# Two-layer pooling and attention backbone: the first gate's conditioning as four 1 MB pieces between the mixer's groups, and the first MLP weights cast in two halves

## The chip, the core and the metric

The kernel runs on one core of one Trainium2 chip. The metric is the device time of one execution in microseconds (us); the median of three runs before the change is 1172.9 us (1172.45 to 1174.26).

Five engines work side by side, each in the order of its own instruction list: PE (matmul), PEld (the weight loads of PE), DVE (vector), ACT (scalar), POOL, and SP, which here only issues transfers. They wait for each other by semaphores.

## The reference, cut to what matters

Two layers over 512 latent and 256 context rows of width 1024. Every sub-layer is modulated by shift, scale and gate vectors that a linear map makes out of a conditioning vector. Layer 0 mixes tokens by centred means, layer 1 by attention; each is followed by a squared-ReLU MLP.

```python
def ada_mods(cond, w, b):
    m = (jax.nn.silu(cond) @ w + b)[..., None, :]
    return jnp.split(m, N_MOD, axis=-1)          # sh1, sc1, gt1, sh2, sc2, gt2
...
        h_lat = modulate(rms_norm(x, g_mix_pre[i]), sh1, sc1)
...
            y_lat = pool_mixer(h_lat, w_pool[j], pool_scale[j])
...
        x = x + gt1 * rms_norm(y_lat, g_mix_post[i])
        m_lat = sq_relu_mlp(modulate(rms_norm(x, g_mlp_pre[i]), sh2, sc2), w_mlp_in[i], w_mlp_out[i])
```

## The kernel before, in words

Rows are kept in six tiles of 128 (tiles 0 to 3 latent, 4 and 5 context). Every large product is made of three fp32r matmuls (high by high, high by low, low by high), so each operand is split: ACT casts it to fp32r (the high part) and DVE subtracts that from the original (the low part). The helper `split` does this.

The first 100 us are the first stage: layer 0's norm, conditioning, pooling mixer, gate and residual, and the first part of the MLP. It is a list of steps with times written out by hand (class `Steps`, `st.at(time, function, ...)`); the list is sorted by time and the functions called in that order. The times are only an order: up to 48 (PE) and 47.3 (DVE, ACT) the engines keep exactly the order of the list (line 65 in the profile); behind that a scheduler may reorder, by its own estimate of durations.

The conditioning of layer 0 is read from HBM in 1 MB blocks (`raw_load`, line 123, issued by SP in list order) into four buffers. For each piece three steps follow:

- `ada_mm` (line 219) multiplies the blocks with the conditioning vector, into one PSUM bank `psada`. A piece of width 4 has two blocks, each with four matmuls of 128 x 512 that fill the four 32-row quarters of the bank (in the trace each such fp32 matmul is two records); width 2 has one block with eight matmuls of 128 x 256.
- `ada_rows` transposes the bank on DVE into `work` or `rows`.
- `ada_sel` sums and turns it by four small matmuls (`work,sel` or `rows,sel`) into the same bank, and `ada_out` adds the bias on DVE into `mods`. Only then is the bank free.

The bank comes from the pool `psB` of four banks, which the context part of the centred means (`psc`), the context mixer's results (`pspool`, tile 4), the gate rows (`psg`) and transposes (`psx`) share. A buffer of a 1 MB block is free again when its last matmul has read it.

The mixer: `centred` makes the operands `ra` (ACT high, DVE low) for eight column blocks k, `pool_a(t, (g,))` does the six 128 x 256 matmuls of tile t and group g (k = 2g, 2g+1) into `pspool`. The gate GT1 then goes through `gate_rows`: DVE multiplies `mods` by a gain into `gc`, four matmuls spread it over the rows (`psg`), ACT copies that to `gate`. DVE multiplies it into the mixer's result (line 326) and adds to the residual stream `xr` (line 329).

After that, per tile pair: `turn0` transposes on PE (`psx`, line 379), `mod0` applies shift and scale on ACT (line 389) and DVE (line 391) and splits (ACT line 395, DVE line 396), and `parts0` does the first MLP product (`psin`, line 567). The first MLP weights arrive in one 1 MB block; before, one `split` makes `rb` of all 2048 columns (ACT line 142, DVE line 145). From about 125 us on the MLP runs in groups on PE (lines 817 and 691).

What the change touches: the body of `ada_mm`, the loop over `CONDITIONING` that puts these steps in the list, one time of the second piece of SC2/SH2 (`landing`), and the step of `split(*raws[0])`.

Of the kernel before, what the change touches and what calls it, by code (L numbers as in the profile page):

```python
# [9 lines left out]
F32 = mybir.dt.float32  # L10
# [7 lines left out]
P = 128  # L18
D = 1024
KT = D // P  # L20
# [14 lines left out]
SH1, SC1, GT1, SH2, SC2, GT2 = range(6)  # L35
# [33 lines left out]
def backbone(ctx: ExitStack, tc, x, ctx_in, w_ada, w_pool, pool_scale, w_qkv, g_q, g_k, w_o, w_mlp_in,  # L69
# [21 lines left out]
    psB = ctx.enter_context(tc.tile_pool(name="psB", bufs=4, space=PSUM))  # L91
# [29 lines left out]
    def raw_load(src, pool=None):  # L121
        t = (pool or pools[0]).tile([P, 2048], F32, tag="raw", name="raw")
        d = sy.dma_start(t, src)
        if pinned[0]:
            tc.keep_in_program_order(d)
        return t
# [12 lines left out]
    def split(raw, hi, lo, pin=False, q=None):  # L139
        if q is not None:  # L140
            raw, hi, lo = (z[:, 512 * q:512 * q + 512] for z in (raw, hi, lo))
        a = sc.copy(hi, raw)  # L142
        if pin:
            tc.keep_in_program_order(a)
        b = ve.tensor_tensor(out=lo, in0=raw, in1=hi, op=ALU.subtract)  # L145
        if pin:
            tc.keep_in_program_order(b)
# [68 lines left out]

    rowsd, parts, seeded, stale = {}, {}, {}, [0]

    def ada_mm(i, m, j, w=2):
        ps = psB.tile([P, 512], F32, tag="b", name="psada")  # L220
        kn = 2048 // (w * P)
        for z in range(KT // kn):
            raw = raw_load(w_ada[i, m, j + z]).rearrange("p (k n) -> p k n", n=w * P)
            for k in range(kn):
                at = kn * z + k
                q = 32 * (at % 4)
                te.matmul(ps[q:q + 32, 0:w * P], cond[:, at, :], raw[:, k, :], start=(at < 4), stop=(at >= 4))  # L227
        rowsd[i, m, j] = ps, w

    def ada_rows(i, m, j):  # L230
        ps, w = rowsd[i, m, j]
# [489 lines left out]
    def w_in(i, g, rg, pin=False, wait=None):  # L721
        return rg.load(w_mlp_in[i, g], 256, pin, wait)
# [4 lines left out]
    st = Steps()  # L727
    for t in range(NT):
        st.at(4.6 + 1.3 * t, rows_a, t)
    landing = ((19.3, 21.4, 22.4), (23.8, 25.9, 27), (27.1, 28.15, 28.7), (28.9, 30.0, 30.5), (31.4, 32.4, 33.4),  # L730
               (33.7, 34.8, 35.2), (40.6, 42.65, 43.9), (44.2, 46.25, 47.2),
               (47.75, 48.5, 49.5), (52.8, 53.2, 54.7), (60.5, 61.5, 62), (62.9, 63.9, 64.4), (65.2, 66.2, 66.7), (67.7, 68.7, 69.2))
    for zs, (m, j, w) in zip(landing, CONDITIONING):
        for z, fn, also in zip(zs, (ada_mm, ada_rows, ada_sel), ((w,), (), ())):
            st.at(z, fn, 0, m, j, *also)
    st.at(0, ordered.__setitem__, 0, True)
    st.at(0, mixed.__setitem__, 0, True)
    st.at(47.3, mixed.__setitem__, 0, False)
# [25 lines left out]
        st.at((23.4, 24.4)[h], pool_split, h, False)  # L764
    raws = []
    st.at(62.95, lambda: first.append(Inner(0, w_in(0, 0, ring, False, raws), hH, hL, hids0[0], chunks0, TOK)))
    st.at(63.2, lambda: split(*raws[0]))
    for h in range(2):
        for ci in range(2):
            st.at(((47.65, 46.2), (47.7, 47.6))[h][ci], gate_rows, 0, GT1, ci, (h,))  # L770
# [4 lines left out]
    for n, t in enumerate(order):  # L775
        b = 50.5 + 2.9 * n
# [685 lines left out]
```

## Time and profile before

| what | value |
|---|---|
| median of three runs | 1172.9 us |
| the profiled execution's own time / its span | 1173.48 / 1171.7 us |
| PE busy in the span | 1143.0 us (98%) |
| DVE, ACT, POOL busy | 938.4, 636.7, 67.0 us |
| mean granted PE clock | 0.996 of full |
| PE busy, 30 to 40 / 40 to 50 / 50 to 60 us | 7.48 / 9.30 / 9.42 of 10 us |
| PE clock in the same stretches | 0.97 / 0.69 / 1.00 |

A row of the timeline gives the start in us, the time until the last of the merged instructions ended, engine, line, operation, output and inputs, shapes, how many records, and in brackets the idle time before it with what ended it. Records of matmuls overlap, so the time a group takes on PE is read from its start to the start of the next group. Line 65 stands for every step whose order is pinned.

### The profile page before, as it was taken

To read this page: it belongs to the slowest core of one execution; us is meant where nothing else is said; L and a number is where in the kernel's file an instruction comes from. 1 tells how busy PE (TensorE), PEld (TensorE's weight loads), DVE (VectorE), ACT (ScalarE), POOL (GpSimd) and SP (SyncE) were. 2 spreads that over 40 slices of the span, in tenths; PEclk is the share of its full clock that TensorE was granted. 3 is DMA by queue.
4 is the path that set the end of the run, shared out by engine and by line. 5 is a ranking of instruction groups with operands and counts; after the bars stand their busy time and mean duration, and the time that the engine had idled before them with its cause. 6 is when DMAs were issued, how large, how long until landed. Compare 5 with 4: busy or idle time off the path is not lost.

```text
span 1171.7 us, 15966 instructions
## 1 busy us (share of the span) xinstructions
PE 1143.0 (98%) x6172; PEld 989.2 (84%) x6172; DVE 938.4 (80%) x1538; ACT 636.7 (54%) x1082; POOL 67.0 (6%) x120
## 2 busy tenths in 40 slices
PE   7899999999999999999999999999899999999997
PEld 5579899889899988998887889988888888888886
DVE  4688687989988997996778599877787779778876
ACT  4577655555454534555675388852776436535522
POOL 2030000000000000000241200001100000000001
PEclk9899999999999999999999999999999999999999
DMA  9884213343334334343423101115234124314312
GB/s 375 354 318 154 72 45 135 133 159 109 144 144 144 144 137 147 112 144 108 180 73 107 37 1 37 37 73 197 91 138 150 61 84 144 108 36 144 108 37 107
DMA packets 25516, 147.32 MB, mean 126 GB/s; under 512 B 2785, under 2 KB 5217, under 8 KB 9698
## 3 DMA queue, kind: packets, MB, share of 16 engines
q1 hardware_dynamic: 25442, 146.32, 34.2%
q8 instruction: 48, 0.79, 0.3%
q14 instruction: 26, 0.21, 0.1%
HBM read 138.96 MB, written 7.34 MB: 125 GB/s over the span
## 4 chain that ended last, share of the span: by engine, by line
PE 49%; issue 42%; POOL 3%; DVE 2%; ACT 2%; DMA 1%; SPq 0%; POOLq 0%; DVEq 0%; ACTq 0%
PE pso L817 22%; PE psin L691 18%; PE psin L567 3%; PE psq L1064 2%; PE pspool L65 1%; POOL rs L185 1%; PE psada L65 1%; PE pspool L490 1%; POOL rs L1073 1%; DMA raw<-in_w_ada 1%; DMA xr<-in_x 1%; PE psada L227 1%; POOL ms L183 1%; DVE ra L65 0%; ACT junk L170 0%
## 5 line engine op out<-in xcount | busy, mean ns | idle before, releaser
L817 PE MATMUL pso<-units,rb 128*128 128x512 f32 x1152 | 278.2, 392 | 0.0
L817 PEld LDWEIGHTS pso<-units,rb 128*128 128x128 f32 x1152 | 214.8, 188 | 41.2
L273 DVE SCALAR_TENSOR_TENSOR rows<-raw,cond,rows 128x256 f32<-128x256 f32 x280 | 126.5, 475 | 2.0
L829 DVE TENSOR_TENSOR acc<-acc,pso 128x512 f32<-128x512 f32 x129 | 85.1, 674 | 41.4 <-PE pso L817 41.2
L567 PE MATMUL psin<-ra,rb 128*128 128x512 f32 (+1 forms) x432 | 103.3, 340 | 1.8 <-ACT ra L364 1.6
L921 PE MATMUL pso<-units,pairs 128*128 128x512 f32 x336 | 82.3, 389 | 0.0
L567 PE MATMUL psin<-ra 128*128 128x512 f32 x256 | 80.5, 390 | 0.0
L567 PEld LDWEIGHTS psin<-ra,rb 128*128 128x128 f32 x432 | 69.9, 189 | 11.3 <-ACT ra L364 1.9
L921 PEld LDWEIGHTS pso<-units,pairs 128*128 128x128 f32 x336 | 63.1, 188 | 13.1
L925 DVE TENSOR_TENSOR acc<-acc,pso 128x512 f32<-128x512 f32 x72 | 48.7, 681 | 28.8 <-PE pso L921 28.8
L183 POOL TENSOR_SCALAR ms<-ss 128x1 f32<-128x1 f32 x20 | 11.4, 572 | 998.3 <-ACT junk L170 946.1
L691 PE MATMUL psin<-ra,units 128*128 128x384 f32 x336 | 65.5, 337 | 0.4 <-ACT psin L703 0.4
L691 PE MATMUL psin<-sums,units 128*128 128x384 f32 x336 | 63.9, 337 | 0.0
L691 PEld LDWEIGHTS psin<-ra,units 128*128 128x128 f32 x336 | 59.7, 188 | 3.9 <-ACT psin L703 0.9
L691 PEld LDWEIGHTS psin<-sums,units 128*128 128x128 f32 x336 | 58.9, 188 | 1.7
L145 DVE TENSOR_TENSOR units<-raw,units 128x1024 fp32r<-128x1024 f32 (+2 forms) x49 | 55.1, 1148 | 4.5 <-ACT units L142 4.4
L567 PEld LDWEIGHTS psin<-ra 128*128 128x128 f32 x256 | 48.0, 188 | 10.0
L142 ACT CAST units<-raw 128x1024 fp32r<-128x1024 f32 (+2 forms) x49 | 46.8, 994 | 14.0 <-PE pso L817 10.2
L827 ACT COPY acc<-pso 128x512 f32<-128x512 f32 x48 | 27.2, 588 | 48.9 <-PE pso L817 48.6
L567 PE MATMUL psin<-rb 128*128 128x512 f32 (+1 forms) x144 | 52.6, 367 | 0.2 <-DVE rb L365 0.2
L1064 PE MATMUL psq<-units,ra 128*128 128x512 f32 x216 | 51.7, 392 | 0.0
L567 PE MATMUL psin<-rb,ra 128*128 128x512 f32 x128 | 49.8, 389 | 0.0
(279 smaller groups left out, 2346.7 us busy)
## 6 DMA issues: line engine op xcount, KB each, us to landing
raw<-in_w_ada SPq DMA_DIRECT2D x48, 1024.0 KB, 4.9
raw<-in_w_mlp_in SPq DMA_DIRECT2D x32, 1024.0 KB, 4.9
raw<-in_w_mlp_out SPq DMA_DIRECT2D x32, 1024.0 KB, 5.3
raw<-in_w_qkv SPq DMA_DIRECT2D x6, 1024.0 KB, 4.8
spill<-xr SPq DMA_DIRECT2D x10, 512.0 KB, 4.2
xr<-spill SPq DMA_DIRECT2D x10, 512.0 KB, 6.8
raw<-in_w_o SPq DMA_DIRECT2D x4, 1024.0 KB, 4.8
xr<-in_x SPq DMA_DIRECT2D x4, 512.0 KB, 5.2
```

The lines of the kernel that those rows point to most:

```text
L65: return lambda *args, **kw: self.tc.keep_in_program_order(f(*args, **kw))
L142: a = sc.copy(hi, raw)
L145: b = ve.tensor_tensor(out=lo, in0=raw, in1=hi, op=ALU.subtract)
L273: ve.scalar_tensor_tensor(out=r, in0=raw[:, k, :], scalar=cond[:, k, c:c + 1], in1=r, op0=ALU.mult, op1=ALU.add)
L567: te.matmul(ps[:, bank, o:o + ln], w[:, k, fs], rhs, start=start, stop=(k == KT - 1 and n == 2), skip_group_check=len(ks) < KT)
L691: te.matmul(bank, w[k], a[k], start=start and k == 0 and m == 0, stop=stop and k == 3 and m == 2, skip_group_check=True)
L817: te.matmul(pss[h][:, 0:cols[h][1]], a[:, f, ts_], w[:, f, cols[h][0]:sum(cols[h])], start=(n == 0 and not seeded[t]), stop=(n == len(seq) ...
L827: sc.copy(d, ps)
L829: ve.tensor_tensor(out=d, in0=d, in1=ps[:, 0:w], op=ALU.add)
L921: te.matmul(ps, a, w, start=(m == 0), stop=(m == len(seq) - 1))
L925: ve.tensor_tensor(out=M[n][:, t], in0=M[n][:, t], in1=ps, op=ALU.add)
L1064: te.matmul(ps, a[:, k, sl], w[:, k % 4, :], start=(k == 0 and n == 0), stop=(k == KT - 1 and n == 2))
```

## The change

For the gate GT1 (two pieces of width 4, so four blocks) `ada_mm` is no longer called once per piece with both blocks, but once per block. The first piece's blocks stand at 35.3 and 36.25 in the list, the second's at 40.6 and 42.61; before, the two whole pieces stood at 40.6 and 44.2. `ada_rows` and `ada_sel` stay where they were (42.65 and 43.9; 46.25 and 47.2). The whole piece SH2 of columns 0 to 511 moves from 52.8 to 52.5 in the list. The split of the first MLP weights becomes two steps of 1024 columns. Bytes, matmuls and their operands stay the same; ACT and DVE have one instruction more each.

```diff
-    def ada_mm(i, m, j, w=2):
-        ps = psB.tile([P, 512], F32, tag="b", name="psada")
-        kn = 2048 // (w * P)
-        for z in range(KT // kn):
+    def ada_mm(i, m, j, w=2, zs=None):
+        if (i, m, j) not in rowsd:
+            rowsd[i, m, j] = psB.tile([P, 512], F32, tag="b", name="psada"), w
+        ps, kn = rowsd[i, m, j][0], 2048 // (w * P)
+        for z in range(KT // kn) if zs is None else zs:
             raw = raw_load(w_ada[i, m, j + z]).rearrange("p (k n) -> p k n", n=w * P)
...
-        rowsd[i, m, j] = ps, w
...
-               (47.75, 48.5, 49.5), (52.8, 53.2, 54.7), (60.5, 61.5, 62), (62.9, 63.9, 64.4), (65.2, 66.2, 66.7), (67.7, 68.7, 69.2))
+               (47.75, 48.5, 49.5), (52.5, 53.2, 54.7), (60.5, 61.5, 62), (62.9, 63.9, 64.4), (65.2, 66.2, 66.7), (67.7, 68.7, 69.2))
     for zs, (m, j, w) in zip(landing, CONDITIONING):
         for z, fn, also in zip(zs, (ada_mm, ada_rows, ada_sel), ((w,), (), ())):
-            st.at(z, fn, 0, m, j, *also)
+            if m != GT1 or fn != ada_mm:
+                st.at(z, fn, 0, m, j, *also)
+        if m == GT1:
+            for z in range(2):
+                st.at(((35.3, 36.25), (40.6, 42.61))[j // 2][z], ada_mm, 0, m, j, w, (z,))
...
-    st.at(63.2, lambda: split(*raws[0]))
+    for h in range(2):
+        st.at((63.2, 63.55)[h], lambda h: split(*(z[:, 1024 * h:1024 * h + 1024] for z in raws[0])), h)
```

On PE, in the pinned part, the mixer's groups and the gate stood like this before (`pspool` the mixer, `psada<-raw` the blocks of GT1, `psada<-work,sel` their turning, `psg` the gate rows):

```order
L65 MATMUL pspool<-rb,ra 128x256 x24
L65 MATMUL psada<-raw,cond 32x512 x8
L65 MATMUL pspool<-rb,ra 128x256 x12
L65 MATMUL psada<-work,sel 32x2x4 x4
L65 MATMUL psada<-raw,cond 32x512 x8
L65 MATMUL psg<-ident,gc 128x128 x4
L65 MATMUL psada<-work,sel 32x2x4 x4
L65 MATMUL psg<-ident,gc 128x128 x12
```

The same place on PE with the change:

```order
L65 MATMUL psada<-raw,cond 32x512 x4
L65 MATMUL pspool<-rb,ra 128x256 x12
L65 MATMUL psada<-raw,cond 32x512 x4
L65 MATMUL pspool<-rb,ra 128x256 x12
L65 MATMUL psada<-raw,cond 32x512 x4
L65 MATMUL pspool<-rb,ra 128x256 x6
L65 MATMUL psada<-raw,cond 32x512 x4
L65 MATMUL pspool<-rb,ra 128x256 x6
L65 MATMUL psada<-work,sel 32x2x4 x4
L65 MATMUL psg<-ident,gc 128x128 x4
L65 MATMUL psada<-work,sel 32x2x4 x4
L65 MATMUL psg<-ident,gc 128x128 x12
```

All four blocks now stand ahead of the last mixer group, and between the first turning and the first `psg` nothing is left; before, eight block matmuls stood there. The first block takes the bank that `psc` of k = 4, 5 leaves, the mixer's second bank that of the last SH1 piece; before, the mixer had the former and GT1 the latter.

Some 10 us later on PE, where the order is the scheduler's, the piece SH2 (line 227) before stood whole behind tile 1's mixer (line 490):

```order
L490 MATMUL pspool<-rb,ra 128x256 x8
L238 MATMUL psada<-work,sel 32x2x4 x4
L490 MATMUL pspool<-rb,ra 128x256 x16
L227 MATMUL psada<-raw,cond 32x512 x8
L379 MATMUL psx<-ident,acc 128x128 x8
```

With the change (the matmul of `ada_mm` is now line 228):

```order
L228 MATMUL psada<-raw,cond 32x512 x4
L490 MATMUL pspool<-rb,ra 128x256 x3
L238 MATMUL psada<-work,sel 32x2x4 x4
L490 MATMUL pspool<-rb,ra 128x256 x6
L228 MATMUL psada<-raw,cond 32x512 x4
L490 MATMUL pspool<-rb,ra 128x256 x15
```

Its two blocks are moved ahead of and into the mixer's tile 1.

On DVE, where the first MLP weights are split, the order before was (391 and 396 the modulated rows, 233 and 249 the conditioning, 326 and 329 gate and residual):

```order
L391 TENSOR_SCALAR acc<-psx,avec_94,mods_91 128x2x128 x2
L233 STREAM_TRANSPOSE rows<-psada 128x256 x2
L145 TENSOR_TENSOR rb<-raw,rb 128x2048
L249 TENSOR_TENSOR mods_91<-psada,vec 128x4 x2
L396 TENSOR_TENSOR ra<-acc,ra 128x4x128 x2
L258 SCALAR_TENSOR_TENSOR avec_94<-mods_91,vec 128x4
L326 TENSOR_TENSOR acc<-pspool,gate 128x512 x2
```

And with the change:

```order
L391 TENSOR_SCALAR acc<-psx,avec_94,mods_91 128x2x128 x2
L233 STREAM_TRANSPOSE rows<-psada 128x256
L145 TENSOR_TENSOR rb<-raw,rb 128x1024 x2
L326 TENSOR_TENSOR acc<-pspool,gate 128x512 x2
L396 TENSOR_TENSOR ra<-acc,ra 128x4x128 x2
L249 TENSOR_TENSOR mods_91<-psada,vec 128x4
L233 STREAM_TRANSPOSE rows<-psada 128x256
L329 SCALAR_TENSOR_TENSOR xr<-acc,rs,xr 128x1024
```

The two halves stand directly behind each other, and the gating of a mixer tile (line 326) has moved ahead of `mods` and of the modulated rows' low part. From about 145 us on the orders of both kernels are the same on every engine; SP's and POOL's are the same throughout.

## The prediction

> **What bounds the kernel now.** I began with the busy times of the page.
>
> ```profile
> PE 1143.0 (98%) x6172; PEld 989.2 (84%) x6172; DVE 938.4 (80%) x1538; ACT 636.7 (54%) x1082; POOL 67.0 (6%) x120
> ```
>
> PE is busy for all but 29 us of the span, so only time on PE counts: idle time in front of it, or work that takes longer. The second view is the waits of PE in the stretch that the change touches, 38 to 140 us.
>
> ```profile
> PE pspool L65 <- DVE mods L65: 0.8, 1, 0.8
> PE psada L227 <- DVE mods L249: 0.7, 1, 0.7
> PE psg L65 <- DVE gc L292: 0.6, 1, 0.6
> PE psada L65 <- DVE rows L65: 0.6, 1, 0.6
> PE psada L65 <- DVE mods L65: 0.3, 1, 0.3
> ```
>
> Five waits, 3.0 us in all, every one for DVE; none is for a transfer. That is the first thing against a gain: blocks that land earlier shorten nothing on PE here. The third view is PE's timeline through the place itself.
>
> ```profile
> 39.58 0.29 PE L65 MATMUL psada<-rows,sel 128*32 128x4 f32 x8 [0.57 <-DVE rows L65]
> 40.70 5.46 PE L65 MATMUL pspool<-rb,ra 128*128 128x256 f32 x24 [0.83 <-DVE mods L65]
> 46.09 1.96 PE L65 MATMUL psada<-raw,cond 128*32 128x512 f32 x16
> 47.97 1.69 PE L65 MATMUL pspool<-rb,ra 128*128 128x256 f32 x12
> 49.59 0.25 PE L65 MATMUL psada<-work,sel 128*32 128x8 f32 x8
> 49.68 1.90 PE L65 MATMUL psada<-raw,cond 128*32 128x512 f32 x16
> 51.51 1.16 PE L65 MATMUL psg<-ident,gc 128*128 128x128 f32 x8
> 52.60 0.25 PE L65 MATMUL psada<-work,sel 128*32 128x8 f32 x8
> 53.42 0.35 PE L65 MATMUL psg<-ident,gc 128*128 128x128 f32 x1 [0.58 <-DVE gc L292]
> ...
> 56.27 1.92 PE L65 MATMUL psada<-raw,cond 128*32 128x512 f32 x16
> 58.12 3.13 PE L65 MATMUL pspool<-rb,ra 128*128 128x256 f32 x24
> ```
>
> Two things show. The 24 mixer matmuls at 40.70 take 5.46 us (0.228 each), while 24 equal ones at 58.12 take 3.13 (0.130). And from 40.70 to 53.42 there is only one gap, 0.58 us. The fourth view tells why the first 24 are slow: the granted clock in short windows (the number behind POOL).
>
> ```profile
> 39.20:39.40 0.20, 0.00 (x0) 0.00 (x0) 0.20 (x1) 0.00 (x0) 0.00 (x0) 0.95 0.70 287
> 39.40:39.60 0.20, 0.02 (x3) 0.02 (x4) 0.20 (x2) 0.00 (x0) 0.00 (x0) 0.50 1.17 492
> ...
> 46.00:46.20 0.20, 0.20 (x5) 0.12 (x8) 0.00 (x0) 0.00 (x0) 0.00 (x0) 0.50 0.00 0
> 46.20:46.40 0.20, 0.20 (x4) 0.07 (x8) 0.00 (x0) 0.00 (x0) 0.00 (x0) 0.98 0.00 0
> ```
>
> PE runs at half clock from 39.4 to 46.2, 6.8 us, and that ends nearly together with the slow 24. Halving that stretch again, with windows of 3.4 us, gives PE's activity before and in it.
>
> ```profile
> 36.00:39.40 3.40, 1.91 (x28) 0.83 (x26) 2.69 (x8) 0.52 (x2) 0.00 (x0) 1.00 1.01 407
> 39.40:42.80 3.40, 2.39 (x18) 2.33 (x19) 1.39 (x6) 1.95 (x4) 0.00 (x0) 0.50 1.02 422
> 42.80:46.20 3.40, 3.40 (x20) 3.17 (x23) 2.18 (x4) 0.99 (x3) 0.00 (x0) 0.50 0.44 183
> ```
>
> After 3.4 us with PE 56% busy the clock falls; after 70% it stays down; after 100% it is back.
>
> **The change part by part.**
>
> *The first block.* It is to run before the mixer's 24, and PE is idle 0.83 us there. But its bank is the one that the context means of k = 4, 5 leave, and DVE reads that last in this row:
>
> ```profile
> 40.08 0.47 DVE L65 SCALAR_TENSOR_TENSOR ra<-psc,avec,ra 128x256 fp32r<-128x256 f32 x1
> 40.47 0.15 DVE L65 TENSOR_TENSOR mods<-psada,vec 128x4 f32<-128x4 f32 x1
> ```
>
> That ends at 40.55, the same instruction that the mixer waits for before. So the first block starts at 40.70 too, the gap stays, and the mixer slides behind the block: 0 us. Its four matmuls leave no new wait for the bytes either: 1 MB takes 1.05 MB / 420 GB/s = 2.5 us, the four blocks of GT1 are the last before the transfers dry up, and they are needed over 10 us.
>
> ```profile
> 44.00:46.00 2.00, 2.00 (x11) 1.86 (x9) 0.98 (x2) 0.00 (x0) 0.00 (x0) 0.50 0.15 61
> 46.00:48.00 2.00, 2.00 (x18) 0.46 (x17) 0.00 (x0) 0.00 (x0) 0.00 (x0) 0.95 0.00 0
> ```
>
> Landed at 46 at the latest, the fourth; the others by an estimate of 2.5 us each at about 43.5, 41 and 38.5. They are wanted at about 50, 48, 45 and 40.7.
>
> *Blocks in halves.* A piece that runs in one go costs 46.09 to 47.97 = 1.88 and 49.68 to 51.51 = 1.83 us. A single block followed by other work is this:
>
> ```profile
> 26.49 1.06 PE L65 MATMUL psada<-raw,cond 128*32 128x512 f32 x8 [2.06 <-DMA raw<-in_w_ada]
> 27.49 0.73 PE L65 MATMUL psc<-gate,acc 128*128 128x136 f32 x4
> ```
>
> 1.00 us. Four of them are 4.00 against 3.71: +0.29. SH2's first piece, which the scheduler now parts too, adds about 0.14 by the same rows. Bounds: 0 and 0.6.
>
> *The turning.* Before, the turning at 49.59 is followed after 0.09 us by the second piece's matmuls, and while they run (1.83 us) DVE makes `mods` and `gc`; the gate rows at 51.51 find them ready. Now nothing is left to put there. The price of the bare chain stands at the second turning: 52.60 to 53.42, 0.82 us from turning to gate rows. So +0.73. DVE's queue adds nothing: the second transpose, 0.72 us, stands behind `gc` and is done while the first gate rows run (1.09 us). Bounds: 0.6 and 0.9.
>
> *The clock.* Everything up to 39.4 is as before, so the clock falls as before. In the slow stretch now stand a block, 12 mixer matmuls and most of another block. How a block runs at half clock no row shows: between 1.0 us (not slowed) and 2.0 (twice). Not slowed, two blocks and 12 mixer matmuls need 1.00 + 12 x 0.228 + 1.00 = 4.74 us of the 5.50 from 40.70 to 46.2, and the last 0.76 slow three more mixer matmuls: 1.00 + 1.00 + 15 x 0.130 = 4.0 us of full-speed work are done, where 24 mixer matmuls are 3.1, a gain of 0.9. Twice: 2.00 + 2.74 and 0.76 of the second block, 1.00 + 1.56 + 0.38 = 2.9, a loss of 0.2. By the mixer's ratio, the nearest row, 0.228 / 0.130 = 1.75: 1.75 + 2.74 and 1.01 of the second block, 3.1, so 0. I take 0 and keep -0.9 to +0.2.
>
> [...]
>
> *Buffers and transfers.* The first block's buffer comes free before the mixer's 24 instead of behind them, so SP can issue the next loads earlier. They are SC2's, whose matmuls start at 56.27 without a wait. 0 us.
>
> *The halved split.* Before, it holds DVE for 2.25 us and PE waits 0.69 us behind it:
>
> ```profile
> 76.51 2.25 DVE L145 TENSOR_TENSOR rb<-raw,rb 128x2048 fp32r<-128x2048 f32 x1
> ...
> 77.81 0.38 PE L567 MATMUL psin<-ra,rb 128*128 128x256 f32 x1
> 78.89 1.07 PE L227 MATMUL psada<-raw,cond 128*32 128x256 f32 x16 [0.69 <-DVE mods L249]
> ```
>
> Two halves cost 2 x 1.2 on DVE and 1.05 instead of 1.90 us on ACT before DVE can begin, by rows of the first stage and of the cast itself:
>
> ```profile
> 21.27 1.05 ACT L65 CAST rb<-raw 128x1024 fp32r<-128x1024 f32 x1 [2.29 <-DVE raw L65]
> ...
> 23.16 2.35 DVE L65 TENSOR_TENSOR rb<-raw,rb 128x1024 fp32r<-128x1024 f32 x2
> ...
> 71.05 0.60 ACT L170 ACTIVATE junk<-pspool 128x512 bf16<-128x512 f32 x1
> ...
> 71.77 1.06 ACT L170 ACTIVATE junk<-xr 128x1024 bf16<-128x1024 f32 x1
> ...
> 73.73 1.90 ACT L142 CAST rb<-raw 128x2048 fp32r<-128x2048 f32 x1
> ```
>
> ACT's cast moves ahead of these two squares (0.7 and 1.1 us to the next start), so with a gate 1.2 us late it begins near 73.73 + 1.2 - 1.8 = 73.1, and DVE's first half near 74.2. But in the new order nothing that PE waits for stands between the halves, and behind them come two gatings before the low part and `mods`:
>
> ```profile
> 78.82 1.28 DVE L396 TENSOR_TENSOR ra<-acc,ra 128x512 fp32r<-128x512 f32 x2
> ...
> 80.09 1.28 DVE L326 TENSOR_TENSOR acc<-pspool,gate 128x512 f32<-128x512 f32 x2
> ```
>
> 2.4 + 1.28 + 0.64 = 4.3 us later, at 78.5, the first low part is there, which the first `psin` needs. PE came to `psin` at 77.81, and is now 1.2 us late there but has eight small instructions less ahead of it, also some 1.2 us: 77.8. A wait of 0.7 us for the 0.69 that goes: 0. I add 0.2 for the waits on banks that a fuller DVE may bring behind that. Bounds for both: -0.7 (no wait at all) and +2 (DVE as late as 4.3 us behind a cast that does not move up).
>
> *Sum*: 0.29 + 0.14 + 0.73 + 0 + 0.2 = +1.36, say +1.3 us. Nothing later takes it back: from 80 us on PE has no wait to fill in the list above, and the orders are soon the same. On the profiled execution, 1173.48 us (span 1171.7 and 1.8 around it), that is 1174.8; this execution lies 0.6 above the median of the three, so I forecast **1174.2 us**. A measurement of this kernel can tell about 0.2%, 2.3 us, from no change, so this is "within".
>
> **The rivals.**
>
> *The clock stays down (slower).* It came back after a window full of mixer matmuls, and not after one that was 70% busy. In the window that ends at 46.2 about 0.8 us are now a block, whose matmuls fill only 32 columns each (the 128*32 of the rows); should those not count, the window is 77% busy. Each further window at half clock costs 3.4 / 2 = 1.7 us, and the next is mixed as well: one to three give 1175.9 to 1179.3 us. Against it: from 46.1 on before, blocks and mixer were mixed and the clock held. It decides at whether 77% restores. 15%.
>
> *The clock is back a window earlier.* A busier PE from 39.4 to 42.8 would save 1.7 us: 1174.2 - 1.7 = 1172.5. Against it: the same 0.83 gap stays in that window, since the first block cannot start earlier. 12%.
>
> *DVE is late by more.* If the 4.3 us of DVE come behind a cast that ACT starts 1.8 us later than I put it, the full +2: 1176.2. For it: DVE is the only engine that PE waits for here. 12%.
>
> *The schedule gives the waits back.* If the scheduler's new order wins all of the 0.69 us, DVE's earlier gatings spare other waits and blocks are not slowed by the clock: 1.16 - 0.7 - 0.9 = -0.4, and with the turning covered by DVE running ahead, up to -2: 1171 to 1172.5. 7%.
>
> That the change does not do what it says is partly in the forecast: the first block is ahead of the mixer in the list and gains nothing there.
>
> **How the numbers follow.** The forecast has 54%, its own range 1173 to 1175.2. Faster by over 0.2% (below 1170.6) needs the last rival at its end with luck in the clock: 7%. Slower by over 0.2% (above 1175.2) has the 15% of the clock, most of the 12% of DVE and a small tail: 27%. The rest is 66%. The range is 1171.3 to 1177.4: it holds the forecast, both small gains, DVE's +2 and one or two windows of slow clock.
>
> **What would show it.** In the changed profile: the first block of GT1 starts at 40.7 on PE with the same wait before it; the second `psg` group (53.42 before) starts near 54.6; the first turning is followed by a wait of about 0.6 us for DVE `gc`; the clock is back at 3.4 us steps, and each step late is 1.7 us; PE's wait for DVE near 77 is there again, under `psin` instead of `psada`. I am wrong if the block starts before 40, if `psg` is earlier than 53.4, or if PE waits for a transfer.

## The result, and the profile after

The changed kernel takes 1176.9 us (median; 1175.1 to 1178.5) where the kernel before, beside it, takes 1173.0 us (1172.5 to 1175.3): a ratio of 1.0027, 95% interval 1.0019 to 1.0036. (The ratio is not that of the two medians: it amounts to 3.2 us, between 2.2 and 4.2.) It is slower by 0.3%, just past the 0.2% that can be told from no change. The forecast had the direction, and +1.3 us for what is +3.9 by the medians. The profiled executions lie 4.1 us apart:

| what | before | after |
|---|---|---|
| profiled execution / its span, us | 1173.48 / 1171.7 | 1177.55 / 1175.8 |
| mean granted PE clock | 0.996 | 0.996 |
| second group of gate rows starts on PE, us | 53.42 | 55.16 |
| first wide `psin` (128x384) starts, us | 102.87 | 106.75 |
| first `pso` starts, us | 119.52 | 123.53 |

The busy times of the changed kernel, the line that answers to the first one shown of before:

```profile
PE 1145.2 (97%) x6172; PEld 988.3 (84%) x6172; DVE 938.6 (80%) x1539; ACT 636.4 (54%) x1083; POOL 68.7 (6%) x120
```

PE has the same 6172 records as before; of the 4.1 us of span 2.2 are PE time and 1.9 are idle time. So both things that the prediction named, work that takes longer and waits, have grown. PE's timeline in the changed place (start, us until the group's last end, engine, line, operation, tiles, shapes, records, idle time ahead):

```profile
40.76 1.93 PE L65 MATMUL psada<-raw,cond 128*32 128x512 f32 x8 [0.76 <-DVE ra L65]
42.62 2.93 PE L65 MATMUL pspool<-rb,ra 128*128 128x256 f32 x12
45.48 1.61 PE L65 MATMUL psada<-raw,cond 128*32 128x512 f32 x8
47.02 1.70 PE L65 MATMUL pspool<-rb,ra 128*128 128x256 f32 x12
...
52.45 0.25 PE L65 MATMUL psada<-work,sel 128*32 128x8 f32 x8
53.27 1.13 PE L65 MATMUL psg<-ident,gc 128*128 128x128 f32 x8 [0.57 <-DVE gc L65]
...
55.16 2.92 PE L65 MATMUL psg<-ident,gc 128*128 128x128 f32 x24 [0.58 <-DVE gc L292]
```

The first block starts where the forecast put it, with its wait; the turning at 52.45 has nothing behind it and costs 52.45 to 53.27 = 0.82 us, as priced. The second group is 1.74 us later than before, where the terms up to there (blocks +0.29, turning +0.73, clock 0) made 1.0. What comes behind adds 2.3 us more until `pso`. PE's waits from 38 to 140 us, in total, times and longest:

```profile
PE psin L567 <- ACT work L574: 0.9, 1, 0.9
...
PE psin L567 <- ACT junk L170: 0.6, 1, 0.6
...
PE psg L65 <- DVE gc L65: 0.6, 1, 0.6
...
PE psin L567 <- DVE ra L396: 0.6, 3, 0.2
PE psada L228 <- DVE acc L391: 0.4, 1, 0.4
```

The 0.6 for `junk` is the wait that was to replace the 0.69 for `mods`; the 0.9, the second 0.6 (`ra`) and the 0.4, together 1.9, are new, and they were priced at 0.2. The largest is at the end of the first MLP product, on PE:

```profile
99.72 0.60 PE L379 MATMUL psx<-ident,acc 128*128 128x128 f32 x4
...
102.93 2.90 PE L567 MATMUL psin<-ra,rb 128*128 128x256 f32 x22 [0.18 <-DVE ra L396]
106.75 16.93 PE L567 MATMUL psin<-ra,units 128*128 128x384 f32 x96 [0.93 <-ACT work L574]
```

and on ACT, which has all four casts of `units` in front of the relu (line 574):

```profile
102.05 3.89 ACT L142 CAST units<-raw 128x1024 fp32r<-128x1024 f32 x4
105.85 1.61 ACT L574 ACTIVATE work<-psin 128x512 f32<-128x512 f32 x4
```

Here is the same place before, PE and then ACT:

```profile
95.02 0.60 PE L379 MATMUL psx<-ident,acc 128*128 128x128 f32 x4
95.37 7.66 PE L567 MATMUL psin<-ra,rb 128*128 128x256 f32 x60
```

```profile
98.57 2.00 ACT L142 CAST units<-raw 128x1024 fp32r<-128x1024 f32 x2
101.75 0.87 ACT L574 ACTIVATE work<-psin 128x512 f32<-128x512 f32 x2 [1.18 <-PE psin L567]
102.51 2.00 ACT L142 CAST units<-raw 128x1024 fp32r<-128x1024 f32 x2
```

Before, 60 narrow matmuls stood behind the last transposes (`psx`), so that no operand is waited for, and only two casts stood ahead of the relu. After, 36 stand there, PE waits twice among them for `ra`, and the wide `psin` waits for the relu.

One thing about reading the times that follow. The mean granted clock differs between executions of the same kernel. In the two profiled executions above there is a stretch of 6.8 us at half clock near 40 us (39.4 to 46.2 and 39.8 to 46.6; the mean from 38 to 56 us is 0.81 in both), in that of the halves alone a shorter one (0.91 from 38 to 56 us), in that of the blocks alone none (1.00); their mean granted clocks over the span are 0.996, 0.997 and 0.999. The mean does not say where a stretch stands: the profiled execution of the row at 52.5 alone has 0.996 as well, with 1.00 from 38 to 56 us and a stretch near 80 us. The changed kernel takes 1177.6 to 1178.5 us at 0.996 (four executions of eight) and 1175.1 to 1175.2 at 0.999 (three); the kernel before has 0.999 in none of the 102 executions that the experiments are compared with. So a median mixes executions of different clocks, and more so for some kernels than for others.

Kernels are compared by their medians and, beside that, at the same mean clock; the table has all of them, and the last two columns are medians of the executions with that clock, some of very few. Two kernels have several executions at a still lower clock, 0.993, that pull their medians up: the row at 52.5 alone three of five (1177.9 to 1178.9), and the last block behind four of twelve (1177.6 to 1178.7).

| kernel | median | ratio to before, 95% interval | at clock 0.996 | at 0.999 |
|---|---|---|---|---|
| before | 1173.0 to 1173.5 | | 1173.99 | none (0.997: 1172.7) |
| changed | 1176.94 | 1.0027 [1.0019, 1.0036] | 1178.09 | 1175.13 |
| halves alone | 1172.54 | 0.9994 [0.9986, 1.0003] | 1173.61 | none (0.997: 1172.43) |
| blocks alone | 1174.76 | 1.0003 [0.9994, 1.0012] | 1174.91 | 1172.14 |
| changed without halves | 1176.50 | 1.0024 [1.0015, 1.0032] | 1177.88 | 1174.74 |
| changed, PE kept busy | 1178.22 | 1.0036 [1.0025, 1.0046] | 1178.90 | 1175.75 |
| changed, row at 52.8 | 1173.32 | 1.0002 [0.9991, 1.0013] | none | 1172.49 |
| changed, casts behind | 1175.70 | 1.0019 [1.0010, 1.0028] | 1176.95 | 1174.39 |
| changed, last block behind | 1174.99 | 1.0015 [1.0003, 1.0027] | 1174.99 | 1172.20 |
| row at 52.5 alone | 1177.89 | 1.0031 [1.0019, 1.0043] | 1175.62 (one) | none |
| halves, piece behind tile 0 | 1173.25 | 0.9997 [0.9988, 1.0006] | 1175.09 | 1172.05 |
| halves, mixer behind turning | 1174.10 | 1.0007 [0.9998, 1.0016] | 1174.83 | 1172.94 (one) |
| halves, both | 1174.51 | 1.0005 [0.9996, 1.0014] | 1175.15 | 1172.19 |
| halves, piece and casts | 1172.66 | 0.9994 [0.9985, 1.0003] | 1173.50 | none (0.997: 1172.29) |

### The profile page after: what moved, and what is told of

It reads as the page before. It is cut to its first block, busy times and chain, and to the rows that moved or that the text cites. A ratio compares the mean times of both kernels' runs of the same rounds, so it can differ in the third digit from the quotient of the medians.

```text
span 1175.8 us, 15970 instructions
## 1 busy us (share of the span) xinstructions
PE 1145.2 (97%) x6172; PEld 988.3 (84%) x6172; DVE 938.6 (80%) x1539; ACT 636.4 (54%) x1083; POOL 68.7 (6%) x120
## 4 chain that ended last, share of the span: by engine, by line
PE 53%; issue 33%; DVE 5%; ACT 3%; POOL 3%; DMA 1%; SPq 0%; POOLq 0%; DVEq 0%; ACTq 0%
PE pso L822 22%; PE psin L691 18%; PE po L1281 2%; PE psy L1307 2%; PE psin L567 2%; PE psq L1069 2%; PE pss L1242 2%; POOL rs L185 1%; PE psada L65 1%; POOL rs L1078 1%; DVE sm L1246 1%; DMA raw<-in_w_ada 1%; PE pspt L1267 1%; PE pspool L65 1%; DMA xr<-in_x 1%
## 5 line engine op out<-in xcount | busy, mean ns | idle before, releaser
L567 PE MATMUL psin<-rb 128*128 128x512 f32 (+1 forms) x144 | 52.6, 367 | 0.2 <-DVE rb L365 0.2
```

Source lines behind the costliest of these rows:

```text
L567: te.matmul(ps[:, bank, o:o + ln], w[:, k, fs], rhs, start=start, stop=(k == KT - 1 and n == 2), skip_group_check=len(ks) < KT)
```

## The experiments

The theory after the two traces (A): 1.7 us lie in the pinned part, some 2 us in the order that the scheduler writes behind it, and the halves cost nothing. Its rivals: the halves make DVE late (B), or the clock makes the difference (C). "The row" is the line of `landing` that places the piece SH2, 52.8 before and 52.5 in the change; TensorE in the expectations is PE.

### Halves alone

```diff
-    st.at(63.2, lambda: split(*raws[0]))
+    for h in range(2):
+        st.at((63.2, 63.55)[h], lambda h: split(*(z[:, 1024 * h:1024 * h + 1024] for z in raws[0])), h)
```

> The kernel before with the first MLP weights cast in two halves and nothing else. Theory A (order): the late waits of the changed kernel come from the order of the instructions behind the pinned part, the halves cost nothing that the end sees: within 0.5 us of the kernel before, ratio 1.000, second group psg at 53.4 us and first wide psin where it was, near 102.9 us. Rival B (halves): the two-piece subtraction on DVE is what makes the waits behind 78 us, so this kernel alone is about 2 us slower, ratio 1.0015 to 1.002.

1172.54 us, ratio 0.9994: A holds. The second group of gate rows starts at 52.35 and `pso` at 118.13. Both are earlier than before, but in an execution with a higher clock ahead of them (0.91 from 38 to 56 us for 0.81); from 56 to 140 us both have 1.00, and the time between the two starts is 65.78 us for 66.10 before. So nothing comes late. The wait for `mods` shrinks from 0.69 to 0.26. B is out for this order of instructions.

### Blocks alone

```diff
         for z, fn, also in zip(zs, (ada_mm, ada_rows, ada_sel), ((w,), (), ())):
-            st.at(z, fn, 0, m, j, *also)
+            if m != GT1 or fn != ada_mm:
+                st.at(z, fn, 0, m, j, *also)
+        if m == GT1:
+            for z in range(2):
+                st.at(((35.3, 36.25), (40.6, 42.61))[j // 2][z], ada_mm, 0, m, j, w, (z,))
```

(The body of `ada_mm` is that of the change.)

> The kernel before with GT1 conditioned in four blocks and nothing else (last cut of the row still at 52.8, weights cast whole). Both theories: the second group psg starts 1.7 us later than before, near 55.2 us. Theory A (order): the 1.7 us stay, and what comes behind depends on the order that the scheduler writes; the last transposes stand early here, as in the kernel before, so the first wide psin comes 1.7 to 2.5 us later than 102.9 us, and the time is 1.5 to 2.5 us above before, less than the changed kernel's 3.9. Rival B (halves): also 1.7 us. Rival C (clock): in executions without the half-clock stretch the blocks cost under 1 us, ratio 1.0005 to 1.001.

1174.76 us, ratio 1.0003; at clock 0.996 1174.91, 0.9 above before. That is under the 1.5 us at which A's range began, so A is right about the kind and not about the size. The order behind takes some back, as its rows show: from the piece SC2 (55.37) to `pso` (118.14) it needs 62.77 us, before 56.27 to 119.52 = 63.25.

This execution has no stretch at half clock, and so gives clean prices for the pinned part (PE, kernel with the blocks alone):

```profile
40.77 1.06 PE L65 MATMUL psada<-raw,cond 128*32 128x512 f32 x8 [0.78 <-DVE ra L65]
41.77 1.70 PE L65 MATMUL pspool<-rb,ra 128*128 128x256 f32 x12
43.39 1.07 PE L65 MATMUL psada<-raw,cond 128*32 128x512 f32 x8
...
47.01 0.98 PE L65 MATMUL pspool<-rb,ra 128*128 128x256 f32 x6
47.92 1.07 PE L65 MATMUL psada<-raw,cond 128*32 128x512 f32 x8
...
49.82 0.25 PE L65 MATMUL psada<-work,sel 128*32 128x8 f32 x8
50.64 1.13 PE L65 MATMUL psg<-ident,gc 128*128 128x128 f32 x8 [0.58 <-DVE gc L65]
...
52.53 2.92 PE L65 MATMUL psg<-ident,gc 128*128 128x128 f32 x24 [0.58 <-DVE gc L292]
```

The order of before at full clock stands in the profile of a later experiment, the row at 52.5 alone, which leaves the pinned part as it was:

```profile
40.73 3.11 PE L65 MATMUL pspool<-rb,ra 128*128 128x256 f32 x24 [0.87 <-DVE mods L65]
43.77 1.92 PE L65 MATMUL psada<-raw,cond 128*32 128x512 f32 x16
45.62 1.69 PE L65 MATMUL pspool<-rb,ra 128*128 128x256 f32 x12
47.24 0.25 PE L65 MATMUL psada<-work,sel 128*32 128x8 f32 x8
47.32 1.90 PE L65 MATMUL psada<-raw,cond 128*32 128x512 f32 x16
...
51.07 2.92 PE L65 MATMUL psg<-ident,gc 128*128 128x128 f32 x24 [0.58 <-DVE gc L292]
```

From start to start, the blocks take four times 1.00 for 1.85 + 1.84: +0.3. The mixer takes 1.62 + 1.62 + 0.91 + 0.91 = 5.06 in four groups for 3.04 + 1.62 = 4.66 in two: +0.4. The first turning takes 0.82 for 0.08: +0.74. Together 52.53 - 40.77 = 11.76 for 51.07 - 40.73 = 10.34: +1.42. The 0.4 is what the forecast left out: it priced the parted blocks, and not the mixer's groups that they part. In the two profiled executions with the stretch it is 1.68, so the clock adds 0.26: a block at half clock takes 40.76 to 42.62 = 1.86 us, nearly twice its 1.00.

### The change without the halves

```diff
-    for h in range(2):
-        st.at((63.2, 63.55)[h], lambda h: split(*(z[:, 1024 * h:1024 * h + 1024] for z in raws[0])), h)
+    st.at(63.2, lambda: split(*raws[0]))
```

> The changed kernel with the first MLP weights cast whole again; its TensorE order stays as in the changed kernel but for two rows. Theory A (order): no different from the changed kernel within 0.5 us, ratio to before 1.003, first wide psin near 106.7 us. Rival B (halves): the waits behind 78 us go, 2 us faster than the changed kernel, ratio 1.001 to 1.0015.

1176.50 us, ratio 1.0024; 0.2 below the changed kernel at clock 0.996 and 0.4 at 0.999. A holds, and B is out here too. The three late waits (0.93 for the relu, 0.5 for `ra`, 0.3 for `acc`) are all there. Against the kernel with the blocks alone only one number in the list differs, 52.5 for 52.8, and that makes 2.6 us at 0.999 and 3.0 at 0.996.

### PE kept busy ahead of the stretch

```diff
+    def warm(ps, n):
+        for _ in range(n):
+            te.matmul(ps[:, 256:512], hH[:, 0, 0:P], wp3H[:, 0, :], start=True, stop=True)
...
+        if (i, m, j) == (0, SH1, 3):
+            warm(ps, 5)
...
+    for z, m, n in ((31.41, SC1, 6),):
+        st.at(z, lambda m, n: warm(rowsd[0, m, 3][0], n), m, n)
```

> The changed kernel with 11 more matmuls of 128x256 (fp32r) in TensorE's idle stretches between 35 and 41 us, written into columns of the psada tile that nobody reads, so that TensorE is busy there. Theory C (clock): the fall to half clock near 39.7 us does not come, a block of GT1 takes 1.06 us where it took 1.93, the second group psg starts 2.5 to 3 us earlier than in the changed kernel, and the time is 1174.0 to 1174.5 in every execution, not in some. If the idle time is not what lowers the clock, the rows keep 1.93 and the time 1176 to 1177. Theory A (order): even at full clock the 2 us of waits behind 58 us stay, since the order behind is that of the changed kernel.

1178.22 us: the clock is 0.996 in five executions of nine and 0.999 in four, much as in the changed kernel (four and three of eight). The dummies cost 0.6 to 0.8 us and don't keep the clock up, so C's cure fails. C itself is out as well: at the same clock, 0.996, the changed kernel and the kernel before are still 4.1 us apart. At 0.999 the late waits are there (1.2, 0.9 and 0.4 us), as A has it. That the idle stretches have nothing to do with the fall doesn't follow: the dummies hardly filled them. Of the 3.4 us from 36.0 to 39.4 PE is busy 2.14 us with them and 2.06 without, and from 37.0 to 40.4 1.66 with and 1.90 without.

### The changed kernel with the row back at 52.8

```diff
-               (47.75, 48.5, 49.5), (52.5, 53.2, 54.7), (60.5, 61.5, 62), (62.9, 63.9, 64.4), (65.2, 66.2, 66.7), (67.7, 68.7, 69.2))
+               (47.75, 48.5, 49.5), (52.8, 53.2, 54.7), (60.5, 61.5, 62), (62.9, 63.9, 64.4), (65.2, 66.2, 66.7), (67.7, 68.7, 69.2))
```

> The changed kernel with the row of SH2 back at 52.8 in the list; blocks and halves stay. The scheduler then writes an order in which SH2 stands whole behind the mixer's tile 1 again, the last transposes stand ahead of the last 70 narrow psin matmuls, and only two of the four casts of units stand on ACT ahead of the relu. Theory A (order): no wait for the relu, no third wait for ra, about 2.5 us faster than the changed kernel, close to the kernel with the blocks alone: 1174.7 us in the executions of clock 0.996, ratio to before 1.0005 to 1.001. Rival D (the blocks, with halves, push DVE and ACT late whatever the order): 1177 to 1178 in those executions, as the changed kernel.

1173.32 us, ratio 1.0002 [0.9991, 1.0013]; at 0.999 it is 1172.49 for 1175.13, 2.6 us less than the changed kernel; none of its executions has the clock 0.996 that the expectation speaks of. A holds, the rival D is out. So one number in the list carries most of the loss. What it does: 52.5 puts the piece SH2 ahead of the mixer of tile 1, which stands at 52.6. In the changed kernel tile 1's mixer is cut up by the piece's blocks (line 228) and ends late:

```profile
59.85 3.14 PE L65 MATMUL pspool<-rb,ra 128*128 128x256 f32 x24
62.92 1.06 PE L228 MATMUL psada<-raw,cond 128*32 128x512 f32 x8
63.92 0.62 PE L490 MATMUL pspool<-rb,ra 128*128 128x256 f32 x3
...
66.55 2.05 PE L490 MATMUL pspool<-rb,ra 128*128 128x256 f32 x15
```

and DVE, which multiplies the gate into it (the second line 326 here), stands idle ahead of it:

```profile
65.45 1.29 DVE L326 TENSOR_TENSOR acc<-pspool,gate 128x512 f32<-128x512 f32 x2 [0.29 <-ACT junk L170]
...
70.14 1.29 DVE L326 TENSOR_TENSOR acc<-pspool,gate 128x512 f32<-128x512 f32 x2 [1.57 <-ACT junk L170]
```

With the row at 52.8 it follows without a wait, 8.18 us after tile 0's mixer began (57.14) where the changed kernel needs 10.29:

```profile
62.73 1.29 DVE L326 TENSOR_TENSOR acc<-pspool,gate 128x512 f32<-128x512 f32 x2 [0.89 <-ACT junk L170]
...
65.32 1.28 DVE L326 TENSOR_TENSOR acc<-pspool,gate 128x512 f32<-128x512 f32 x2
```

Waits are only about half of it. From the second group of gate rows to `pso`, at full clock in both traces, the changed kernel needs 68.37 us and this one 65.60. Of these 2.8 us PE is idle for 1.5 (2.59 for 1.10) and busy for 1.3 more (65.78 for 64.50) with the same matmuls. The kernels without the halves show it again, with the row at 52.5 and at 52.8: 68.45 us for 65.61, busy 65.88 for 64.67. That the longer work comes from groups that part each other, as in the rows above, is read from the order; no run isolates it.

### The changed kernel with two casts behind the relu

```diff
-        wo_ = w_out(0, 0, one(unit[2]))
+        wo_ = w_out(0, 0, one(unit[2]), True)
```

> The changed kernel with the split of the first output weights pinned, so that two of the four casts of units stand on ACT behind the relu; PE's order differs in 21 rows. Theory A (order): the wait of the first wide psin for the relu (0.9 us) goes or shrinks to 0.2, 0.7 to 0.9 us faster than the changed kernel at the same clock (1177.2 for 1178.1 at 0.996), the other waits stay. Rival E (the last transposes alone): the relu is late because its psin are late, not because of the casts, and nothing changes: within 0.3 us of the changed kernel.

1175.70 us; at the same clock 0.7 (0.999) to 1.1 us (0.996) under the changed kernel, and the wait for the relu is gone, while the other late waits stay. On ACT there are now two casts, and the relu waits for PE instead of PE for the relu:

```profile
100.78 1.99 ACT L142 CAST units<-raw 128x1024 fp32r<-128x1024 f32 x2
103.27 0.87 ACT L574 ACTIVATE work<-psin 128x512 f32<-128x512 f32 x2 [0.50 <-PE psin L567]
```

A holds, the rival E is out: of the 2.6 us of the row, 0.7 to 1.1 go with ACT's order at the relu. (The pin moves 21 rows of PE's order as well, so this is not a change of ACT alone.)

### The last block behind the first turning

```diff
-                st.at(((35.3, 36.25), (40.6, 42.61))[j // 2][z], ada_mm, 0, m, j, w, (z,))
+                st.at(((35.3, 36.25), (40.6, 44.2))[j // 2][z], ada_mm, 0, m, j, w, (z,))
```

> The changed kernel with the fourth block of GT1 at 44.2 instead of 42.61, behind the first turning. The first turning's chain on DVE is then covered by the block: the wait of 0.58 us ahead of the first psg goes, and the second psg group starts 0.73 us earlier than in the changed kernel at the same clock, near 51.4 us at full clock where the kernel with the blocks alone has 52.53. Behind that the order is the scheduler's and differs: the last transposes stand ahead of 48 narrow psin and two casts ahead of the relu, so by theory A some of the 2.5 us come back too: 1.5 to 3 us faster than the changed kernel. If uncovered turning costs nothing, the second group stays at its place.

The second group starts at 51.62, 10.83 us after the first block where the kernel with the blocks alone needs 11.76: 0.93 less, 0.73 of it the turning (0.09 for 0.82) and 0.2 the two mixer groups of 6 that are one of 12 again. The price of the uncovered turning is shown. The time is 2 us lower by the medians and 3 at the same clock, so the order behind gave back as well, as expected, though four of its twelve executions, at clock 0.993, take as long as the changed kernel; in the profiled one, at 0.999, PE's longest wait is now one of 1.3 us for the norm of a tile (ACT, line 526).

### The row at 52.5 alone

```diff
-               (47.75, 48.5, 49.5), (52.8, 53.2, 54.7), (60.5, 61.5, 62), (62.9, 63.9, 64.4), (65.2, 66.2, 66.7), (67.7, 68.7, 69.2))
+               (47.75, 48.5, 49.5), (52.5, 53.2, 54.7), (60.5, 61.5, 62), (62.9, 63.9, 64.4), (65.2, 66.2, 66.7), (67.7, 68.7, 69.2))
```

> The kernel before with nothing but the row of SH2 at 52.5. SH2 stands in two pieces within the mixer's tile 1, but the last transposes stand early, ahead of 72 narrow psin, and two casts ahead of the relu. Theory A (order, and in it the late last transposes): within 0.7 us of before, since the costly part of the order is not there. Rival F (the early SH2 itself, by its parting or the DVE work that it brings forward): 2 us slower or more.

1177.89 us, ratio 1.0031: A as it stood is wrong here. It had tied the loss to the late last transposes; they are early in this kernel, and it loses too. F has the size, but its wait is another one, on PE:

```profile
PE psx L379 <- ACT acc L526: 3.7, 1, 3.7
```

The transposes of a tile wait 3.7 us for its norm. The way to it begins as in the changed kernel: DVE stands idle 1.11 us ahead of tile 1's gating at 65.76. And another loss follows on PE's idle time: the clock, which did not fall at 40 us in this execution, falls behind it (window, its length, PE busy and records, granted clock, DMA share, GB/s):

```profile
76.00:77.00 1.00, 0.00 (x0) 1.00 0.76 311
...
79.00:80.00 1.00, 1.00 (x18) 0.72 0.06 16
80.00:82.00 2.00, 2.00 (x21) 0.50 0.00 0
82.00:84.00 2.00, 2.00 (x15) 0.79 0.20 82
```

Some 3.4 us at half clock, by an estimate 1.7 us of work (half of it). From the second group of gate rows to `pso` this kernel needs 69.32 us for 66.10 before: 3.2 more, of which 1.7 are that clock. The 4 us by the medians can't be put down to the order alone, since three of the five executions have a clock of 0.993; at 0.996 a single execution is 1.6 us above before. So with the blocks 52.5 for 52.8 costs 2.6 to 3.0 us at the same clock, twice; without them it costs too, through another wait, and how much of that is the clock differs from execution to execution. The new theory (G): a piece of conditioning ahead of a mixer tile leaves DVE idle in front of that tile's gating, and the lost DVE time comes back as waits of PE. It was put to the test from the other side.

### A piece behind a mixer tile, and a covered turning

Three kernels on top of the halves alone. The first moves a piece of SC2 behind tile 0's mixer:

```diff
-               (47.75, 48.5, 49.5), (52.8, 53.2, 54.7), (60.5, 61.5, 62), (62.9, 63.9, 64.4), (65.2, 66.2, 66.7), (67.7, 68.7, 69.2))
+               (47.95, 48.5, 49.5), (52.8, 53.2, 54.7), (60.5, 61.5, 62), (62.9, 63.9, 64.4), (65.2, 66.2, 66.7), (67.7, 68.7, 69.2))
```

> The kernel with the halves alone, and the first piece of SC2 at 47.95 in the list, behind the mixer of tile 0, where it stood at 47.75 ahead of it. Theory G (a piece of conditioning ahead of a mixer tile makes DVE idle in front of that tile's gating, and the lost DVE time comes back later as waits of TensorE): tile 0's mixer is done 1.85 us earlier, DVE's wait of 0.88 us for the square of tile 0 (62.64 us there) goes or moves ahead by over 1 us, DVE is busier between 56 and 70 us, and the time falls by what the piece's own lateness doesn't take back: 0 to 1 us faster than 1172.5. Rival (the order behind is a matter of chance, whatever DVE does): anything from 3 us slower to 1 us faster, without a link to DVE's busy time between 56 and 70 us.

The first half of G holds: DVE's wait of 0.88 us ahead of tile 0's gating is gone, and DVE is busier from 60 to 70 us, 7.89 us for the 6.56 of the halves alone (window, length, DVE busy; first the halves alone, then this kernel):

```profile
60.00:70.00 10.00, 6.56 (x10) 1.00 1.00 404
```

```profile
60.00:70.00 10.00, 7.89 (x14) 1.00 1.01 424
```

The second half falls: the time is 1173.25 us, not below 1172.54, and at clock 0.996 1175.09 (two executions) for 1173.61; from the second group of gate rows to `pso` it takes 67.06 us for the 65.78 of the halves alone. PE waits 0.9 us for the relu and 0.4 for `ra`, with DVE running ahead. An early DVE alone doesn't make the end early; the scheduler's order behind it decides, and G is too simple.

The second moves six mixer matmuls behind the second turning:

```diff
-    for z, t, g in ((30.6, 4, 0), (32.5, 4, 1), (35.4, 4, 2), (36.2, 5, 0), (36.3, 5, 1), (36.4, 5, 2), (42.6, 4, 3), (42.62, 5, 3)):
+    for z, t, g in ((30.6, 4, 0), (32.5, 4, 1), (35.4, 4, 2), (36.2, 5, 0), (36.3, 5, 1), (36.4, 5, 2), (42.6, 4, 3), (47.25, 5, 3)):
...
-        st.at((43.8, 44.6, 54.8, 58, 60.5, 62.8)[n], pool_ms, t)
+        st.at((43.8, 47.26, 54.8, 58, 60.5, 62.8)[n], pool_ms, t)
```

> The kernel with the halves alone, and six of the twelve mixer matmuls (tile 5, last group) moved from ahead of the first turning of GT1 to behind the second, so that they run while DVE makes gc. The uncovered chain of a turning, 0.82 us from turning to gate rows with 0.58 us of wait, is then filled by 0.8 us of matmuls that had to run anyhow: second psg group 0.5 to 0.7 us earlier against the start of the mixer's 24 than in the kernel with the halves alone, 0.6 us faster if the order behind keeps its waits (over 1 us faster or slower if not). If the uncovered turning costs nothing, no change at the second psg group.

```profile
51.57 0.25 PE L65 MATMUL psada<-work,sel 128*32 128x8 f32 x8
51.74 0.98 PE L65 MATMUL pspool<-rb,ra 128*128 128x256 f32 x6
52.56 2.84 PE L65 MATMUL psg<-ident,gc 128*128 128x128 f32 x24
```

The wait of 0.58 us ahead of the second group is gone: 41.39 to 52.56 = 11.17 us, of which the slow 24 mixer matmuls (4.41 for 3.04) are 1.37 of clock, leaves 9.80 for 10.34. That is the 0.5 expected. The kernel is not faster but 1.6 us slower (1174.10; 1.2 at clock 0.996): behind 56 us PE waits 0.94 us for `mods` and runs 3.4 us at half clock near 80 us.

The third has both edits:

> Both edits on top of the halves: SC2's first piece behind the mixer of tile 0, and six mixer matmuls behind the second turning. Theory G with the covered turning: 0.6 us from the turning and 0 to 1 us from the earlier gating, 1171 to 1172 us, faster than both kernels. If either is wrong: 1172.5 or more.

1174.51 us: no gain, as the second line of the expectation has it. The second group starts 11.13 us after the mixer's 24, so the covered turning is there; the waits for the relu (0.9) and the norm (0.7) are too.

### The piece, with two casts behind the relu

The halves, SC2's piece behind tile 0, and the pinned split of above.

> The halves, SC2's first piece behind the mixer of tile 0, and the split of the first output weights pinned, so that two of the four casts of units stand on ACT behind the relu. Theory A: the wait of 0.93 us of the first wide psin for the relu, which stood there with SC2's piece moved, goes as it did from the changed kernel (0.7 us at the same clock), so 0.7 us faster than with the piece alone: 1172.5 where that had 1173.25, and about 1171.3 where the clock does not fall; faster than the kernel before by 0.05 to 0.1%. Rival E (the relu is late for other reasons): the wait stays and the time with it.

1172.66 us, 0.6 below the kernel without the pin; the wait for the relu is gone. So two casts behind the relu help in two different orders, though the pin moves other rows of the order too. The 1171.3 expected for executions without a fall can't be judged: none of the eleven has a clock of 0.999. This kernel and the halves alone are the best ones: both 0.9994 of before, with intervals that reach 1.0003, so they beat the changed kernel by over 4 us and the kernel before by nothing that these measurements can tell.

## Why the prediction was right or wrong

- **The first block, buffers and transfers**: right. The block starts at 40.76 with 0.76 us of wait, for DVE's `ra` as worked out; PE waits for no transfer behind 38 us. (The mixer's wait before is not for the same instruction, as the prediction has it: its row names `mods`, which DVE ends 0.07 us after `ra`.)
- **Blocks in halves, +0.29**: right for the blocks (+0.3), but the same cut parts the mixer's groups, +0.4, which the sum lacked.
- **The turning, +0.73**: right (0.74 at full clock, and again when the last block was put behind it).
- **The clock, 0**: +0.26 between the profiled executions. A block at half clock takes 1.86 us, so the end of "twice" (+0.2) was the true one. (The mixer's ratio of 1.75 came from the lengths of the groups; from start to start it is 0.225 / 0.124 = 1.8.) That the clock falls as before holds for the profiled execution, not for all: three of the changed kernel's eight have a mean clock of 0.999, like the profiled execution of the blocks alone that has no fall, and are 3 us shorter than the four at 0.996.
- **SH2's piece, +0.14**: this is the term that was mis-sized, and the step that failed. It was priced as one more parted piece. Its place ahead of tile 1's mixer costs 2.6 to 3.0 us with the blocks in, by the one number that takes it out (1175.13 to 1172.49 at clock 0.999) and by the one that puts it in (1172.14 to 1174.74).
- **The halved split, +0.2**: the halves themselves give -0.4 to +0.4 at the same clock by the two kernels that isolate them. The chain on DVE was sized well: from the first half to the end of the first low part it takes 75.22 to 79.29 = 4.1 us for the 4.3, and it starts 1.0 us later than was put. But the wait under the first `psin` (0.64 us for 0.7) has the size that was forecast by luck: it ends with ACT's square of a mixer tile (`junk`), and the low part is waited for only 0.15 us behind it. The rival that had DVE late by 2 us had nearly the right size and the wrong place: with the halves in and the row back at 52.8 only 0.4 us is left over the blocks alone (1172.49 for 1172.14), so it was not the cast.
- **The sum**: blocks 0.9 at clock 0.996, row 2.6 to 3.0, halves 0.2 to 0.4 make 3.7 to 4.3 for the measured 3.9. These are three steps of one path from the kernel before to the changed one, so they have to add up; they are not the price of each edit by itself. "Nothing later takes it back" was right: from `pso` to the end the two profiled executions take 1052.2 and 1052.3 us. That the order behind could add was bounded at +2 and taken at 0.2.
- **The range**: that 1176.9 lies in it, below 1177.4, is luck in part. The room above the forecast was left for one or two more windows of slow clock and for a cast that makes DVE late, and neither is what took the time.
- Rivals on the clock: it came back as in the kernel before, after 6.8 us; neither of the two happened. (The steps of 3.4 us by which they were priced were an estimate, half of the one stretch of 6.8 us.) The schedule gave no waits back.

What stays open is how the moved piece leads to the loss. Shown is that it does, that 0.7 to 1.1 us of it go with ACT's order at the relu, that about half is idle time of PE and half longer work, and that idle DVE ahead of tile 1's gating goes with it in two kernels. That the idle DVE is the link was put to the test by SC2's piece and not confirmed. The rest of the 2.6 us (0.6 for `ra`, 0.4 for `acc`, the longer work) is read from the traces and was not taken out one by one.

## What to carry to other kernels

Where part of the order is a scheduler's, price a moved step by where it stands against the steps whose results another engine waits for, not only by its own duration: compare the new order on each engine, and look for a piece that slides in front of a result that is due. Parting a run of matmuls cost on both sides of the cut here, for the work that was put between as well (0.4 us beside 0.3). And change one number at a time: of the three edits in this change, one carried two thirds of the loss and one next to nothing.

## What the runs showed of the hardware

PE was as idle ahead of the stretch in an execution whose clock stayed up as in one whose clock fell. The first line is the kernel with the blocks alone, whose clock stays at 1.00 behind this window; the second is the changed kernel, whose clock is 0.50 from 39.8 to 46.6. Up to 48 us their orders are the same (window, length, PE, PEld, DVE, ACT and POOL busy, granted clock, DMA share, GB/s):

```profile
36.30:39.70 3.40, 1.78 (x27) 0.76 (x25) 2.69 (x8) 0.40 (x1) 0.00 (x0) 1.00 1.02 412
```

```profile
36.30:39.70 3.40, 1.75 (x27) 0.76 (x25) 2.68 (x8) 0.38 (x1) 0.00 (x0) 1.00 1.02 412
```

So the 56% busy in 3.4 us that the prediction took for the cause (51 to 52% in these windows) is not enough of one: of two executions with the same work in front, one falls and one does not. PE's longest wait between 36 and 39.7 us is 0.82 us in the execution that falls and 0.81 in the other, both for DVE's `ra`. What decides between the two no run shows.

The stretches that the windows of the traces show last 6.8 us near 40 us (before and changed, as above) or about 3.4 us near 80 us (the row at 52.5 alone and the mixer behind the turning, as below).

In the last two an idle time of PE came just ahead. In the kernel with the row at 52.5 alone a wait of 3.7 us was followed by about 3.4 us at half clock (79.4 to 82.8 by an estimate from the means of the windows, 1.7 us of work), and in the kernel with the mixer behind the turning a shorter one was too: PE is busy 0.76 us of the 2 from 76 to 78, and the granted clock is 0.66 from 78 to 80, 0.50 to 82, 0.98 to 84 and 1.00 to 86. That the idle time is what lowers the clock no run isolates.
